# Matmul and layer norm, 2048 x 2048 x 2048: another order for the first chunk's arrivals, and two DMA transposes issued later

## The chip, the cores and the metric

The kernel runs on one core of one Trainium2 chip. The metric is the device time of one execution in microseconds (us). Three runs of the kernel before took 245.06, 245.17 and 246.28 us; the median is 245.17 us.

## The reference

```python
x = np.matmul(a, b)                       # a, b: 2048 x 2048 float32
mean = np.mean(x, axis=-1, keepdims=True)
var = np.var(x, axis=-1, keepdims=True)
normalized = (x - mean) / np.sqrt(var + eps)
return (gamma * normalized + beta).astype(np.float32)
```

The kernel multiplies in fp16 with fp32 sums.

## The kernel before, in words

**Tiles.** The contraction K is cut into 16 tiles of 128, M into 16 row blocks of 128, N into four quarters of 512 columns. One matmul (`mm(i, q, kt, ...)`, L85) takes a 128 x 128 piece of A, transposed, as weights and a 128 x 512 piece of B, and adds into one PSUM bank, so there are 16 x 4 x 16 = 1024 of them. PSUM has 8 banks, which accumulators and transposes share (pool `psum`).

**Opening.** B and the first five row blocks (R = 5, rows 0 to 4) arrive while the matmuls already run. The 16 K tiles come in four chunks of four. For chunk 0 the order is: quarter 0 for all five rows, then quarters 1, 2 and 3. The partial sums of quarters 0, 1 and 2 go aside to SBUF on ScalarE (`put_aside`, L264). Quarter 3 runs on through chunks 1 and 2. Then `part(0, 4, 12, ...)` adds tiles 4 to 11 of quarter 0, and VectorE adds the set-aside sums (`add_part`, L268), which frees the banks. `part(1, ...)` does tiles 4 to 15 of quarter 1: tiles 4 to 11 tile by tile over the five rows, then tiles 12 to 15 row by row. `part(2, ...)` does the same for quarter 2. Later the last chunk of quarters 3 and 0 follows, and then rows 5 to 15, one after the other.

**Arrivals.** Every load is fp32 into a staging buffer (pool `stg`, 6 buffers of 128 x 1024) and is then cast to fp16. Chunk 0 of rows 0 to 4 (called A0 to A4; `load_a1`, cast at L186) and tiles 0 to 3 of B in quarter 0 (B0 to B3; `load_b1`, cast at L199) come as nine loads of 256 KB, in the order of the list `arrivals` (L163). All later B comes two tiles at a time, 512 KB (`load_b2`, cast at L205): B6/1 below is the load of tiles 6 and 7 in quarter 1. The casts are on VectorE, for the list `later` (L349) on ScalarE. All these loads are issued by SyncE (SP), in program order. VectorE also works in program order: an `add_part` stands behind the casts of B4/1 and B6/1.

**Transposing A.** Rows 0 to 4 are turned for chunks 0 to 2 on TensorE (`turn`, four 128 x 128 transposes a row, L252, then a ScalarE copy, L254). For chunk 3, `turn_last(i)` (L258) has SP issue a DMA transpose from SBUF to SBUF; T0 to T4 below are those of rows 0 to 4. Their weights are first used by tiles 12 to 15 of `part(1, ...)`. Rows 5 and up are transposed whole by DMA (L346).

**Order around the change.** The order of TensorE's work in chunk 0 is written out by hand (L276 to L294): filler matmuls on zeros, each row's `turn` just after its arrival, and the matmuls between. SP's order behind the opening's loads is B4/1, B6/1, T0, T1, B8/1, T2, T3, B10/1, T4, B12/1, B14/1, B4/2, B6/2 and so on (L349 to L359).

Of the kernel before, what the change touches and what calls it, by code (L numbers as in the profile page):

```python
# [16 lines left out]
def kernel(  # L17
# [19 lines left out]
    KC = 4  # L37
    KW = KC * P
    n_kc = n_kt // KC
    R = 5  # L40
# [32 lines left out]
    def bank(name):  # L73
        return psum.tile([P, NB], FP32, tag="ps", name=name)
# [4 lines left out]
    def at(i):  # L79
        return pair[i // 2][:, i % 2]  # L80

    def mm(i, q, kt, first, last):
        if (i, q) not in acc:
            acc[i, q] = bank(f"acc{i}_{q}")
        nc.tensor.matmul(  # L85
            acc[i, q], at(i)[:, kt, :], b16[:, kt, ds(q * NB, NB)],
            start=first, stop=last,
        )
# [71 lines left out]

    arrivals = [("a", 0), ("b", 0)] + [("a", i) for i in range(1, R)]  # L163
    arrivals += [("b", k) for k in range(1, KC)]

    a16_of = {}
    fresh = {"st": 0}
# [33 lines left out]
    def load_b2(k, q, cast=nc.vector.tensor_copy):  # L201
        st = stg.tile([P, 2, NB], FP32, tag="st", name=f"stb{q}_{k}")
        nc.sync.dma_start(
            st, b[ds(k * P, 2 * P), ds(q * NB, NB)].rearrange("(t p) n -> p t n", p=P))
        cast(b16[:, k:k + 2, ds(q * NB, NB)], st)  # L205
        return st
# [36 lines left out]
    def filler(n, to=None):  # L243
        for _ in range(n):
            nc.tensor.matmul(warm if to is None else to, zeros[:, 0:P], zeros, start=True, stop=True)  # L245

    def turn(rows, c):
        n = len(rows)
        t_ps = psum.tile([P, n, KC, P], FP16, tag="ps", name=f"tps{rows[0]}_{c}")
        for m, i in enumerate(rows):  # L250
            for j in range(KC):
                nc.tensor.transpose(t_ps[:, m, j, :], a16_of[i, c][:, ts(j, P)], ident)  # L252
        i0 = rows[0]
        nc.scalar.copy(  # L254
            pair[i0 // 2][:, ds(i0 % 2, n), ds(c * KC, KC), :], t_ps)

    def turn_last(i):
        nc.sync.dma_start_transpose(at(i)[:, ds(K3, KC), :], a16_of[i, n_kc - 1])  # L258

    def put_aside(p, q):  # L260
        if xs[p] is None:
            xs[p] = xpool.tile([P, N], FP32, tag="x", name=f"x{p}")
            bnst[p] = stat.tile([P, n_nb, 6], FP32, tag="bnst", name=f"bnst{p}")
        nc.scalar.copy(xs[p][:, ds(q * NB, NB)], acc.pop((p, q)))  # L264
# [15 lines left out]
    filler(1)  # L280
    turn([1], 0)
    filler(2)
    for i in range(2, R):
        turn([i], 0)
        mm(i - 1, 0, 0, True, False)
    for p in range(R - 1):
        mm(p, 0, 1, False, False)
    mm(R - 1, 0, 0, True, False)
    mm(R - 1, 0, 1, False, False)
    for kt in range(2, KC):  # L290
        for p in range(R):
            mm(p, 0, kt, False, kt == KC - 1)
            if kt == KC - 1:
                put_aside(p, 0)  # L294


    for q in ASIDE[1:]:
# [40 lines left out]
    def load_row(i):  # L338
        a16[i] = a16p.tile([P, K], FP16, tag="a16", name=f"a16_{i}")
        nc.gpsimd.dma_start(a16[i], a[ts(i, P), :])  # L340
# [9 lines left out]
    later += [(k, 2) for k in range(KC, n_kt, 2)]  # L350
    later += [(k, q) for q in (MAIN, 0) for k in range(K3, n_kt, 2)]
    for n, (k, q) in enumerate(later):
        for i in range(2 * n, min(2 * n + 2, R)):
            turn_last(i)
        st = load_b2(k, q, nc.scalar.copy)
        if (k, q) in ((n_kt - 2, 2), later[-1]):
            nc.gpsimd.tensor_copy(gate, st[:, 0, 0:1])
        if (k, q) == (n_kt - 2, 2):
            load_row(R)  # L359
# [152 lines left out]
```

## Time and profile before

| what | value |
|---|---|
| time, median of 3 runs | 245.17 us |
| the profiled execution's own time | 244.29 us |
| its span, first to last instruction | 242.2 us |
| mean granted TensorE clock | 0.993 |
| matmuls of L85 | 1024 |
| VectorE busy, share of the span | 71% |
| ScalarE busy, share of the span | 27% |
| `at<-a16s` DMA transposes, issue to landing | 6.4 us median (5.7 to 7.1) |
| `stb<-in_b_dram` loads of 512 KB, issue to landing | 7.1 us median (4.5 to 9.6) |

A profile has one row for a group of instructions: start, length, engine, line, operation, output and input, count, and in brackets how long the engine sat idle before and what ended that. Matmul rows overlap: one lasts 0.38 us by the profile, but the next starts long before it ends. So a row of n matmuls lasts n - 1 steps from start to start and 0.38 us more, and a wait shows as a step that is too long.

### The profile page before, as it was taken

To read this page: it belongs to the slowest core of one execution; us is meant where nothing else is said; L and a number is where in the kernel's file an instruction comes from. 1 tells how busy PE (TensorE), PEld (TensorE's weight loads), DVE (VectorE), ACT (ScalarE), POOL (GpSimd) and SP (SyncE) were. 2 spreads that over 40 slices of the span, in tenths; PEclk is the share of its full clock that TensorE was granted. 3 is DMA by queue.
4 is the path that set the end of the run, shared out by engine and by line. 5 is a ranking of instruction groups with operands and counts; after the bars stand their busy time and mean duration, and the time that the engine had idled before them with its cause. 6 is when DMAs were issued, how large, how long until landed. Compare 5 with 4: busy or idle time off the path is not lost.

```text
span 242.2 us, 2970 instructions
## 1 busy us (share of the span) xinstructions
PE 235.4 (97%) x1117; PEld 107.5 (44%) x1117; DVE 171.6 (71%) x300; ACT 66.0 (27%) x115; POOL 12.5 (5%) x20
## 2 busy tenths in 40 slices
PE   7999999999999999999999999999999999999992
PEld 2444554444444444444444444444444444444441
DVE  1554545606359998999999999998858392946761
ACT  2465443146760013020202103112111121112132
POOL 0000000000120001000000000004500000000000
PEclk9999999999999999999999999999999999999997
DMA  5999999999979999948898978999927145130405
GB/s 123 396 387 387 386 384 374 195 344 387 381 137 203 346 209 180 238 180 185 247 229 225 248 162 293 236 201 186 228 81 183 76 117 145 53 120 1 173 0 173
DMA packets 43909, 53.28 MB, mean 220 GB/s; under 512 B 27124, under 2 KB 27124, under 8 KB 43640
## 3 DMA queue, kind: packets, MB, share of 16 engines
q1 hardware_dynamic: 42312, 47.34, 63.7%
q0 software_dynamic: 1584, 5.77, 14.8%
q8 instruction: 8, 0.13, 0.2%
q14 instruction: 5, 0.04, 0.0%
HBM read 35.67 MB, written 16.78 MB: 217 GB/s over the span
## 4 chain that ended last, share of the span: by engine, by line
PE 94%; DMA 2%; ACT 1%; DVE 1%; issue 0%; DVEq 0%
PE acc L85 91%; DMA st<-in_a_dram 2%; PE tps L252 2%; PE warm L245 1%; ACT x L437 1%; DVE bnst L402 0%; DVE x L268 0%; PE y L425 0%; DVE a16s L186 0%; PE ms_ps L420 0%; ACT mv_last L418 0%; DVE mv_last L417 0%; ACT lead L421 0%; DVEq L268 0%
## 5 line engine op out<-in xcount | busy, mean ns | idle before, releaser
L85 PE MATMUL acc<-b,at 128*128 128x512 f16 x1024 | 223.0, 379 | 0.1
L85 PEld LDWEIGHTS <-at 128*128 128x128 f16 x1024 | 99.8, 98 | 120.2 <-ACT at L254 1.1
L96 DVE BATCH_NORM_STATS2 bnst<-x 128x6 f32<-128x512 f32 x43 | 29.4, 687 | 23.0 <-ACT x L95 23.0
L117 DVE SCALAR_TENSOR_TENSOR x<-x,rstd,beta_b 128x512 f32<-128x512 f32 x62 | 44.4, 756 | 0.6
L111 DVE SCALAR_TENSOR_TENSOR x<-x,mv,gamma_b 128x512 f32<-128x512 f32 x60 | 42.9, 756 | 0.0
L95 ACT COPY x<-acc 128x512 f32<-128x512 f32 x43 | 24.5, 585 | 66.9 <-PE acc L85 66.9
L272 DVE TENSOR_TENSOR x<-acc,x 128x512 f32<-128x512 f32 x20 | 13.6, 678 | 13.6 <-PE acc L85 13.6
L106 ACT ACTIVATE sq<-ve 128x1 f32<-128x1 f32 x15 | 3.0, 203 | 65.2 <-DVE ve L104 65.2
L205 DVE CAST b<-stb 128x1024 f16<-128x1024 f32 x16 | 11.1, 694 | 12.5 <-DMA stb<-in_b_dram 12.5
L205 ACT CAST b<-stb 128x1024 f16<-128x1024 f32 x14 | 14.6, 1045 | 16.8 <-DMA stb<-in_b_dram 16.8
L273 DVE BATCH_NORM_STATS2 bnst<-x 128x6 f32<-128x512 f32 x20 | 13.9, 694 | 0.7
L264 ACT COPY x<-acc 128x512 f32<-128x512 f32 x20 | 10.2, 605 | 7.5 <-PE acc L85 7.5
L254 ACT COPY at<-tps 128x512 f16<-128x512 f16 (+1 forms) x11 | 8.1, 742 | 10.8 <-PE tps L252 10.5
L340 POOL DMA_DIRECT2D a<-in_a_dram x11 | 6.0, 548 | 92.9 <-DMA at<-a 92.1
L245 PE MATMUL warm<-zeros 128*128 128x512 f16 x19 | 7.4, 534 | 1.2 <-DVE zeros L152 1.2
L186 DVE CAST a16s<-st 128x512 f16<-128x512 f32 x8 | 3.4, 428 | 5.9 <-DMA st<-in_a_dram 5.7
L194 DVE CAST a16s<-sta 128x1024 f16<-128x1024 f32 x6 | 4.2, 694 | 4.1 <-DMA sta<-in_a_dram 3.4
L386 POOL TENSOR_SCALAR gb<-gb 1x1024 f32<-1x1024 f32 x2 | 5.6, 2829 | 0.0
L252 PEld LDWEIGHTS <-a16s 128*128 128x128 f16 x60 | 4.0, 100 | 3.6 <-DVE a16s L186 2.2
L252 PE MATMUL tps<-ident,a16s 128*128 128x128 f16 x60 | 5.4, 225 | 0.1
L102 DVE BATCH_NORM_AGGREGATE mv<-bnst 128x2 f32<-128x24 f32 x15 | 4.0, 264 | 0.5
L245 PEld LDWEIGHTS <-zeros 128*128 128x128 f16 x19 | 2.2, 127 | 3.9 <-issue 2.5
(33 smaller groups left out, 26.3 us busy)
## 6 DMA issues: line engine op xcount, KB each, us to landing
stb<-in_b_dram SPq DMA_DIRECT2D x30, 512.0 KB, 7.1
out_dram<-x SPq DMA_DIRECT2D x30, 512.0 KB, 4.3
a<-in_a_dram POOLq DMA_DIRECT2D x11, 512.0 KB, 6.2
sta<-in_a_dram SPq DMA_DIRECT2D x6, 512.0 KB, 6.5
st<-in_a_dram SPq DMA_DIRECT2D x8, 256.0 KB, 6.1
st<-in_b_dram SPq DMA_DIRECT2D x4, 256.0 KB, 6.0
gamma_b<-in_gamma_dram SPq DMA_DIRECT2D x1, 1024.0 KB, 5.5
beta_b<-in_beta_dram SPq DMA_DIRECT2D x1, 1024.0 KB, 8.6
```

Of the source, the lines that this page charges most:

```text
L85: nc.tensor.matmul(acc[i, q], at(i)[:, kt, :], b16[:, kt, ds(q * NB, NB)], start=first, stop=last,)
L95: nc.scalar.copy(xs[i][:, qs], acc[i, q])
L96: nc.vector.bn_stats(bnst[i][:, q, :], xs[i][:, qs])
L111: nc.vector.scalar_tensor_tensor(xs[i][:, qs], xs[i][:, qs], mv[:, 0:1], gamma_b[:, qs], AluOp.subtract, AluOp.mult)
L117: nc.vector.scalar_tensor_tensor(xs[i][:, qs], xs[i][:, qs], rstd, beta_b[:, qs], AluOp.mult, AluOp.add)
L205: cast(b16[:, k:k + 2, ds(q * NB, NB)], st)
L245: nc.tensor.matmul(warm if to is None else to, zeros[:, 0:P], zeros, start=True, stop=True)
L252: nc.tensor.transpose(t_ps[:, m, j, :], a16_of[i, c][:, ts(j, P)], ident)
L254: nc.scalar.copy(pair[i0 // 2][:, ds(i0 % 2, n), ds(c * KC, KC), :], t_ps)
L264: nc.scalar.copy(xs[p][:, ds(q * NB, NB)], acc.pop((p, q)))
L272: nc.vector.tensor_tensor(xs[p][:, qs], acc[p, q], xs[p][:, qs], AluOp.add)
L273: nc.vector.bn_stats(bnst[p][:, q, :], xs[p][:, qs])
```

## The change

The nine first loads come in the order A0 B0 A1 A2 A3 B1 B2 A4 B3 instead of A0 B0 A1 A2 A3 A4 B1 B2 B3. TensorE's hand-written order follows: the matmuls of rows 0 to 3 on tiles 1 and 2 stand before row 4's `turn`, and row 4 does its four matmuls last. SP issues T0, B8/1, T1, B10/1, T2, B12/1, B14/1, T3, T4, B4/2, so that at most one transpose stands between two loads of quarter 1, and T3 and T4 stand behind the last of them. The number of instructions of every kind is the same.

```diff
-    arrivals = [("a", 0), ("b", 0)] + [("a", i) for i in range(1, R)]
-    arrivals += [("b", k) for k in range(1, KC)]
+    arrivals = [("a", 0), ("b", 0)] + [("a", i) for i in range(1, R - 1)]
+    arrivals += [("b", 1), ("b", 2), ("a", R - 1), ("b", 3)]
...
-    for i in range(2, R):
+    for i in range(2, R - 1):
         turn([i], 0)
         mm(i - 1, 0, 0, True, False)
+    for p in range(R - 2):
+        mm(p, 0, 1, False, False)
+    for kt in (0, 1):
+        mm(R - 2, 0, kt, kt == 0, False)
+    for p in range(R - 2):
+        mm(p, 0, 2, False, False)
+    turn([R - 1], 0)
+    mm(R - 2, 0, 2, False, False)
     for p in range(R - 1):
-        mm(p, 0, 1, False, False)
-    mm(R - 1, 0, 0, True, False)
-    mm(R - 1, 0, 1, False, False)
-    for kt in range(2, KC):
-        for p in range(R):
-            mm(p, 0, kt, False, kt == KC - 1)
-            if kt == KC - 1:
-                put_aside(p, 0)
+        mm(p, 0, 3, False, True)
+        put_aside(p, 0)
+    for kt in range(KC):
+        mm(R - 1, 0, kt, kt == 0, kt == KC - 1)
+    put_aside(R - 1, 0)
...
     for n, (k, q) in enumerate(later):
-        for i in range(2 * n, min(2 * n + 2, R)):
+        for i in {0: (0,), 1: (1,), 2: (2,), 4: (3, 4)}.get(n, ()):
             turn_last(i)
```

## The prediction

> **What bounds the kernel now.** I read the page first, then the chain that ended last in order of time, then the timelines of single engines at the two places the change touches.
>
> ```profile
> PE 235.4 (97%) x1117; PEld 107.5 (44%) x1117; DVE 171.6 (71%) x300; ACT 66.0 (27%) x115; POOL 12.5 (5%) x20
> ```
>
> TensorE sets the time. Only its waits can be won, so I looked for those in the chain:
>
> ```profile
> 46.50 0.69 DVE x L268
> ...
> 47.24 8.36 PE acc L85 x38
> 55.60 0.04 issue
> 55.64 177.59 PE acc L85 x822
> ```
>
> From 9.97 us to the end of the matmuls at 233.23 us the chain leaves TensorE twice only: at 47.24, which an `add_part` released, and at 55.64. The timeline of TensorE sizes the two waits:
>
> ```profile
> 13.25 11.17 PE L85 MATMUL acc<-b,at 128*128 128x512 f16 x51
> 46.56 1.05 PE L85 MATMUL acc<-b,at 128*128 128x512 f16 x3
> 55.00 1.01 PE L85 MATMUL acc<-b,at 128*128 128x512 f16 x3
> ```
>
> The first row is undisturbed: 50 steps in 11.17 - 0.38 us, 0.216 us a matmul. In the second, two steps take 0.67 instead of 0.43: a wait of 0.24 us before the start at 47.24. In the third, two steps take 0.63: a wait of 0.20 us before 55.64. Counting 0.216 us a matmul from the last `turn` (its chain piece ends at 32.70) puts `part(1)`, row 4, tile 4 at 47.24 and row 0, tile 14 at 55.64. What they waited for:
>
> ```profile
> 42.46 0.69 DVE L205 CAST b<-stb 128x1024 f16<-128x1024 f32 x1 [0.81 <-DMA stb<-in_b_dram]
> 45.29 0.69 DVE L205 CAST b<-stb 128x1024 f16<-128x1024 f32 x1 [2.14 <-DMA stb<-in_b_dram]
> 45.90 3.08 DVE L268 TENSOR_TENSOR x<-acc,x 128x512 f32<-128x512 f32 x5
> ```
> ```profile
> 54.54 1.04 ACT L205 CAST b<-stb 128x1024 f16<-128x1024 f32 x1 [0.75 <-DMA stb<-in_b_dram]
> ```
>
> The bank for row 4 is freed by the second of five adds (46.50 to 47.18). VectorE could have begun the adds when row 0 was summed, about 44.6, but stood 2.14 us waiting for B6/1, whose cast is ahead of them. At 55.64 tile 14 had waited for the cast of B14/1, which ended at 55.58. So both waits come from the B stream, and SP's rows show what stands in it:
>
> ```profile
> 37.67 2.70 SPq L258 DMA_TRANSPOSE at<-a16s  x2
> 40.47 0.53 SPq L203 DMA_DIRECT2D stb<-in_b_dram  x1
> 41.09 4.46 SPq L258 DMA_TRANSPOSE at<-a16s  x2
> 45.60 0.58 SPq L203 DMA_DIRECT2D stb<-in_b_dram  x1
> ```
>
> **Part 1, the opening.** VectorE's casts and TensorE's rows:
>
> ```profile
> 9.09 0.43 DVE L186 CAST a16s<-st 128x512 f16<-128x512 f32 x1 [0.27 <-DMA st<-in_a_dram]
> 9.76 0.43 DVE L199 CAST b<-st 128x512 f16<-128x512 f32 x1 [0.24 <-DMA st<-in_b_dram]
> 10.43 0.43 DVE L199 CAST b<-st 128x512 f16<-128x512 f32 x1 [0.25 <-DMA st<-in_b_dram]
> 11.11 0.43 DVE L199 CAST b<-st 128x512 f16<-128x512 f32 x1 [0.25 <-DMA st<-in_b_dram]
> ```
> ```profile
> 9.29 0.39 PE L85 MATMUL acc<-b,at 128*128 128x512 f16 x1
> 9.57 0.40 PE L252 MATMUL tps<-ident,a16s 128*128 128x128 f16 x4
> 9.95 0.39 PE L85 MATMUL acc<-b,at 128*128 128x512 f16 x1
> ```
>
> The nine loads are alike (256 KB, one every 0.67 us, casts of 0.43 us for A and B), so I let the slots keep their times and change only who sits in them: B1 9.09, B2 9.76, A4 10.43, B3 11.11. Until 9.29 (row 2, tile 0) nothing changes. Before: 9.29, `turn` of row 4 at 9.57, row 3 at 9.95, then row 0, tile 1 at 10.23 (B1's cast ended at 10.18) and 15 more steps of 0.216, so quarter 1 starts at 10.23 + 16 x 0.2156 = 13.68. After: row 0, tile 1 at 9.57 (the slot's cast ends at 9.52, as A4's did for the start at 9.57). From there 17 matmuls and one `turn` follow; eight transposes with nothing waiting move the chain by 0.45 (24.64 to 25.09), so four cost 0.22. 9.57 + 17 x 0.2156 + 0.22 = 13.46. **Gain 0.23 us.** The feeds come in time: B2 cast 10.18, used 10.65; A4 cast 10.86, `turn` 11.30; B3 cast 11.54, used 11.73; row 4's ScalarE copy (0.59, begun 0.2 after the `turn`) ends about 12.3, used 12.59. The set-asides move from 13.02 to about 12.3, nothing waits longer. Quarter 1's first B is cast by 13.17, 0.29 before use. If the slots swap less kindly, a load late by 0.1 costs 0.1 at most 0.23 before the gain is gone.
>
> **Part 2, the B stream.** The order of SP changes, the work does not. The trace's semaphores go round in eight, each transfer waiting for the one eight before. B6/1 was issued at 37.25, T0 follows; B8/1 moves from 40.47 to 39.0, B10/1 from 45.60 to about 41, B12/1 and B14/1 from 47.5 and 48.1 to 43 to 44. T3 must wait for B6/1's landing, about 45, T4 follows, both out by 48; B4/2 is queued behind them, 48 against 48.7 now. T3 and T4 take 5.7 to 7.1 us to land: 52 to 55, while row 3's tile 12 comes at about 57. That slack of 2 us or more hides the move; without it every us late costs one.
>
> When does B14/1 land? Casts started, so loads landed, at 45.29, 47.77 (T0 and T1 between), 50.12 (T2, T3), 52.75 (T4), 54.54, 56.68, then every 1.34. So a transpose costs the stream (2.48 - 1.34)/2 = 0.57 or (2.35 - 1.34)/2 = 0.51, in the worst row 1.29. With three instead of five: 45.1 + 4 x 1.34 + 3 x 0.55 = 52.1, or 54.3 with 1.29 each. Needed is 53.85 (use at 54.96, less 1.04 and 0.06). I take 52.1, since two of three rows lie there. **The wait of 0.20 goes.**
>
> The Trainium skill (Advanced Engine Details and Errata, X-Bar Transpose) says that transposing DMAs run as fast as plain ones, 350 to 400 GB/s; for 128 KB that is an estimate of 0.35 us, and B14/1 would come only 0.7 us earlier, just enough. The rows above say more than 0.5 each.
>
> **B6/1 itself**, the hard term: T0 still follows it, only T1 goes. Bounds: it lands as now (45.29), or as the loads before it did (42.46 + 1.34 = 43.8). In the trace 15 of its 16 completion counts came by 43.72 and the last at 45.27; a code fetch (queue q8, 16 KB) began at 42.28 and took 2.20 us, where the one at 21.39 took 1.05. The fetch follows TensorE's position, 0.23 earlier after the change. I take the row that the last count is nearest to: B6/1 lands about 0.2 earlier, 45.05. Then the wait at 47.24 stays at 0.24 and passes the opening's gain on.
>
> The Trainium skill (DMA: Bandwidth & Descriptors, Queues, rings and completion order) says that a completion count lands only after all earlier writes of its DMA engine, across queues. By that rule the late count hangs on the fetch and not on T1, which is the reading taken here; no row shows which engine made the fetch.
>
> **Sum.** 0.23 + 0.20 = 0.43 us: 244.29 becomes 243.86 for the profiled execution. That one lies 0.88 below the median; on the median, 245.17 - 0.43 = 244.7.
>
> **The rivals.**
> 1. T1 was what held B6/1: it lands by 44.8, both waits go: 0.23 + 0.24 + 0.20 = 0.67, 244.5. For it: packets stood still around T0 and T1 alone, T2 to T4 cost 0.5. Against: the last count and the fetch.
> 2. B6/1 lands at 45.29 whatever comes behind: row 4, tile 4 stays at 47.24, the opening's gain is swallowed there, and 0.20 is left: 245.0. For it: loads before B6/1 keep their places, so nothing upstream moves.
> 3. Slower: each transpose standing alone between loads holds the stream as T0 did. B4/1 to B6/1 took 2.83, 1.49 over 1.34. Three such: 45.05 + 5.36 + 3 x 1.49 = 54.9, and tile 14 starts at 56.0 against 55.64: slower by 0.4, 245.6; with a second hold of 1.5 as at a fetch, 1.9, 247.1. It decides from a landing of B14/1 after 54.54; each us beyond is a us. Against: T1 to T4 cost about 0.5.
> 4. The change does nothing in the opening: B1 in A4's slot lands later by 0.2 or more. Then 0.20 to 0.0, 245.1.
>
> **Numbers.** Forecast 0.42, rival 1 0.22, rival 2 0.13, rival 3 0.13, rival 4 0.06, and 0.04 for a larger gain where timed executions hold longer at B6/1 than the profiled one. Predicted 244.7. The range takes in the bounds 244.5 and 245.1 and the first half of rival 3, and below the forecast as much again as the runs scatter: 244.1 to 245.8. A measurement tells about 0.5% (1.2 us) from no change. No case but the last and the far end of rival 3 passes it: faster 0.08, same 0.83, slower 0.09.
>
> **What would show it.** Right: quarter 1's first matmul at 13.46; no ScalarE cast just before a late step near 55; VectorE's fifth-last cast before the adds starting near 45.05; TensorE's last matmul 0.43 earlier. Wrong: B14/1's cast starting after 54.5, a step over 0.22 in `part(1)` rows 3 and 4 (T3, T4 late), or a wait between 9.6 and 13.4.

## The result, and the profile after

The changed kernel took 244.25 us, the median of 22 runs (243.69 to 245.38); the kernel before took 245.12 beside it (22 runs, 244.2 to 246.39). The ratio is 0.9968, with a 95% interval of 0.9954 to 0.9982: 0.8 us less, 0.4 to 1.1 by the interval. It was compared twice more below (0.9982, 0.9963 to 1.0001, and 0.9983, 0.9960 to 1.0006). Weighted by their intervals the three give 0.9975, about 0.6 us, with some 0.25 to either side if they are taken as independent. That is under 0.5%, to the faster side, as forecast; 0.43 us had been worked out. The median of the kernel before differs from one comparison to the next (244.45 to 245.12 in the four made here) by as much as the change is worth, so only ratios to runs taken beside it are used.

The profile that came with the result is of an execution at the upper end of its runs: 245.38 us, span 242.9 us. Its first line:

```profile
PE 234.3 (96%) x1117; PEld 107.2 (44%) x1117; DVE 171.2 (70%) x300; ACT 65.9 (27%) x115; POOL 12.7 (5%) x20
```

The casts of the opening on VectorE, in the changed order, and TensorE's rows beside them:

```profile
9.04 0.43 DVE L186 CAST a16s<-st 128x512 f16<-128x512 f32 x1 [0.25 <-DMA st<-in_a_dram]
9.72 0.43 DVE L199 CAST b<-st 128x512 f16<-128x512 f32 x1 [0.25 <-DMA st<-in_b_dram]
10.40 0.43 DVE L199 CAST b<-st 128x512 f16<-128x512 f32 x1 [0.25 <-DMA st<-in_b_dram]
11.05 0.43 DVE L186 CAST a16s<-st 128x512 f16<-128x512 f32 x1 [0.23 <-DMA st<-in_a_dram]
11.71 0.43 DVE L199 CAST b<-st 128x512 f16<-128x512 f32 x1 [0.23 <-DMA st<-in_b_dram]
```
```profile
9.53 0.40 PE L252 MATMUL tps<-ident,a16s 128*128 128x128 f16 x4
9.92 2.16 PE L85 MATMUL acc<-b,at 128*128 128x512 f16 x9
11.92 0.39 PE L252 MATMUL tps<-ident,a16s 128*128 128x128 f16 x4
```

The slots are 0.67 us apart as before, with B1 and B2 in the sixth and seventh and A4 in the eighth. The whole row of casts is 0.63 us later than in the profile of before (9.72 against 9.09 for the sixth), because B0 was cast later, at 7.01 instead of 6.37. So this profile can only be read from its own first loads. From 9.92 TensorE does nine matmuls, row 4's `turn` and the next matmuls without a gap, and quarter 1 starts at 14.09: 4.37 us after the sixth cast starts, where it was 13.68 - 9.09, or 4.60 unrounded, before.

Later, in the chain that ended last, and on VectorE and ScalarE at that place:

```profile
46.84 1.29 DVE x L268 x2
48.13 0.04 issue
48.17 185.79 PE acc L85 x860
```
```profile
21.20 0.69 DVE L194 CAST a16s<-sta 128x1024 f16<-128x1024 f32 x1 [0.66 <-DMA sta<-in_a_dram]
24.10 0.69 DVE L205 CAST b<-stb 128x1024 f16<-128x1024 f32 x1 [2.20 <-DMA stb<-in_b_dram]
...
44.85 0.69 DVE L205 CAST b<-stb 128x1024 f16<-128x1024 f32 x1 [0.75 <-DMA stb<-in_b_dram]
46.23 0.69 DVE L205 CAST b<-stb 128x1024 f16<-128x1024 f32 x1 [0.68 <-DMA stb<-in_b_dram]
46.84 3.08 DVE L268 TENSOR_TENSOR x<-acc,x 128x512 f32<-128x512 f32 x5
```
```profile
48.48 1.04 ACT L205 CAST b<-stb 128x1024 f16<-128x1024 f32 x1 [9.56 <-DMA stb<-in_b_dram]
50.04 1.04 ACT L205 CAST b<-stb 128x1024 f16<-128x1024 f32 x1 [0.51 <-DMA stb<-in_b_dram]
51.84 1.04 ACT L205 CAST b<-stb 128x1024 f16<-128x1024 f32 x1 [0.75 <-DMA stb<-in_b_dram]
53.23 1.04 ACT L205 CAST b<-stb 128x1024 f16<-128x1024 f32 x1 [0.35 <-DMA stb<-in_b_dram]
```

The chain leaves TensorE once instead of twice: the wait at row 0, tile 14 is gone, since B14/1's cast, the last of the four on ScalarE (B8/1, B10/1, B12/1, B14/1), starts at 53.23 and tile 14 is only reached after 56. The wait behind the adds is still there, and longer: 0.39 us at row 3, tile 4 and 0.38 at row 4. B6/1 came 1.38 us behind B4/1 (46.23 - 44.85), as plain loads do, against 2.83 before. But the whole stream of loads was late in this execution: behind the cast at 21.20 the next load took 2.9 us to come, where before it took 1.35 and the one after it was held up, for less. From the sixth cast to B6/1's it took 36.51 us here and 36.20 before. That is 0.31 more, TensorE is 0.23 earlier, and the wait of 0.24 should grow to 0.78; the two waits are 0.77 together.

### The profile page after: what moved, and what is told of

The parts are those of the page before. It is cut to its first block, busy times and chain, and to the rows that moved or that the text cites. A ratio compares the mean times of both kernels' runs of the same rounds, so it can differ in the third digit from the quotient of the medians.

```text
span 242.9 us, 2971 instructions
## 1 busy us (share of the span) xinstructions
PE 234.3 (96%) x1117; PEld 107.2 (44%) x1117; DVE 171.2 (70%) x300; ACT 65.9 (27%) x115; POOL 12.7 (5%) x20
## 4 chain that ended last, share of the span: by engine, by line
PE 93%; DMA 2%; DVE 1%; ACT 1%; SPq 0%; issue 0%; DVEq 0%
PE acc L85 91%; DMA st<-in_a_dram 2%; PE tps L252 1%; ACT x L442 1%; DVE x L268 1%; DVE bnst L407 0%; PE y L430 0%; DVE a16s L186 0%; PE warm L245 0%; SPq L198 0%; SPq L184 0%; PE ms_ps L425 0%; ACT mv_last L423 0%; DVE mv_last L422 0%; ACT lead L426 0%
## 5 line engine op out<-in xcount | busy, mean ns | idle before, releaser
L85 PE MATMUL acc<-b,at 128*128 128x512 f16 x1024 | 223.0, 379 | 1.5 <-DVE b L199 1.0
L85 PEld LDWEIGHTS <-at 128*128 128x128 f16 x1024 | 99.7, 98 | 120.5 <-issue 1.2
L117 DVE SCALAR_TENSOR_TENSOR x<-x,rstd,beta_b 128x512 f32<-128x512 f32 x62 | 43.9, 748 | 0.6
L245 PE MATMUL warm<-zeros 128*128 128x512 f16 x19 | 6.5, 476 | 1.2 <-DVE zeros L152 1.2
L194 DVE CAST a16s<-sta 128x1024 f16<-128x1024 f32 x6 | 4.2, 694 | 4.1 <-DMA sta<-in_a_dram 4.1
```

The costliest lines, as they stand in the source:

```text
L85: nc.tensor.matmul(acc[i, q], at(i)[:, kt, :], b16[:, kt, ds(q * NB, NB)], start=first, stop=last,)
L117: nc.vector.scalar_tensor_tensor(xs[i][:, qs], xs[i][:, qs], rstd, beta_b[:, qs], AluOp.mult, AluOp.add)
```

## The experiments

Each was timed in five rounds beside the kernel before, and gave one profile. Three numbers are read from every profile: the time from the start of the sixth cast to quarter 1's first matmul; the time from the start of the cast of rows 2 and 3's chunk 3 (L194, at 39.13 before) to the start of B6/1's cast, four loads later; and TensorE's waits behind quarter 1's first matmul, at tile 4 of rows 3 and 4 and at tile 14 of row 0 (a step less than 0.03 us too long counts as none). The second column says whether the opening, and then the order of the transposes, is the old or the new one.

| kernel | opening, order | sixth cast | to quarter 1 | to B6/1 | waits (row 3, row 4, tile 14) | ratio and interval |
|---|---|---|---|---|---|---|
| before | old, old | 9.09 | 4.60 | 6.16 | 0, 0.24, 0.20 | |
| before again | old, old | 9.52 | 4.61 | 6.00 | 0, 0.11, 0.11 | 1.0011 (0.9992 to 1.0031) |
| opening only | new, old | 9.20 | 4.37 | 6.90 | 1.18, 0.38, 0.25 | 1.0005 (0.9989 to 1.0022) |
| order only | old, new | 9.59 | 4.60 | 5.75 | none | 1.0019 (1.0001 to 1.0038) |
| order only, again | old, new | 9.72 | 4.60 | 5.83 | 0, 0.36, 0 | 0.9994 (0.9969 to 1.0019) |
| after | new, new | 9.72 | 4.37 | 6.06 | 0.39, 0.38, 0 | 0.9968 (0.9954 to 0.9982) |
| after, second | new, new | 9.27 | 4.37 | 5.12 | none | 0.9982 (0.9963 to 1.0001) |
| after, third | new, new | 8.95 | 4.37 | 5.38 | none | 0.9983 (0.9960 to 1.0006) |
| T1 back | new, T1 as before | 9.38 | 4.37 | 6.04 | 0.37, 0.38, 0 | 1.0006 (0.9983 to 1.0029) |
| two plain first | new, T0 behind B10/1 | 9.28 | 4.37 | 5.13 | none | 0.9980 (0.9962 to 0.9997) |
| all behind | new, T0 behind B14/1 | 9.22 | 4.37 | 5.35 | 0.27 at row 5 | 0.9998 (0.9977 to 1.0020) |
| two ahead | new, T0, T1 before B6/1 | 9.40 | 4.37 | 7.84 | 1.67, 0.38, 0 | 1.0108 (1.0077 to 1.0139) |
| cast on ScalarE | new, new | 9.29 | 4.37 | 5.34 | none | 0.9971 (0.9952 to 0.9990) |
| opening, cast on ScalarE | new, old | 9.74 | 4.37 | 5.70 | 0, 0, 0.03 | 0.9990 (0.9959 to 1.0021) |

**The two parts, each alone.** The opening alone keeps the old loop:

```diff
-        for i in {0: (0,), 1: (1,), 2: (2,), 4: (3, 4)}.get(n, ()):
+        for i in range(2 * n, min(2 * n + 2, R)):
```

> Only the first part of the change: arrivals and hand-written order of chunk 0; SP's order of the transposes T0 to T4 as before. Measured from the start of the sixth cast (the slot at 9.09 us before), quarter 1's first matmul should come 4.37 us later instead of 4.59, in every theory. Theory F (as predicted: T0 and the code fetch hold B6/1, and the B stream of quarter 1 still carries all five transposes): the 0.23 us is swallowed in part(1), the waits there grow from 0.44 to about 0.67 us, ratio 0.999 to 1.000. Rival W (in the timed executions the waits of part(1) are mostly not there, the profiled one was unlucky): the 0.23 us is kept, ratio about 0.999. Rival G (the gain of the whole change is bigger than its profile shows because the opening gains more in executions whose first loads come late): ratio 0.997.

The opening's gain is there, 4.37, and nothing of it reaches the end: 1.0005. VectorE's rows of this profile:

```profile
43.59 0.69 DVE L205 CAST b<-stb 128x1024 f16<-128x1024 f32 x1 [0.75 <-DMA stb<-in_b_dram]
46.50 0.69 DVE L205 CAST b<-stb 128x1024 f16<-128x1024 f32 x1 [2.21 <-DMA stb<-in_b_dram]
47.11 3.07 DVE L268 TENSOR_TENSOR x<-acc,x 128x512 f32<-128x512 f32 x5
```

B6/1 comes 2.91 us behind B4/1 as in the profile of before (2.83), and TensorE, which is earlier, waits longer: 1.81 us in all. It is the swallowing that theory F foresaw. Its 0.67 us of waits is too little for this execution, which is the slowest of its runs (246.28 us). The order alone is the kernel before with the new loop:

> Only the second part: SP's order T0, B8/1, T1, B10/1, T2, B12/1, B14/1, T3, T4; the opening as before. Theory F: the wait for B14/1 (0.20 us before) goes, the wait for B6/1 (0.24) stays: 0.2 us, ratio 0.9992, and no step over 0.22 us near part(1), row 0, tile 14. Rival 1 (T1 held B6/1): both waits go, 0.44 us, ratio 0.998. Rival 3 (a transpose alone between loads holds the stream like the first one): B14/1's cast starts after 54.5 and the ratio is over 1.000.

Its profile has no wait: the chain runs from the last `turn` to the last matmul without leaving TensorE,

```profile
33.21 200.09 PE acc L85 x927
```

where before the same 927 matmuls ended at 233.23 from 32.70, 200.53 us: 0.44 more. Yet the runs were no faster: 1.0019, with an interval that lies just above 1. So it was run again.

> The second part alone once more, since its first run (1.0019, 1.0001 to 1.0038) went against its own profile, which has no wait in part(1). Theory T (two transposes one right behind the other are what held B6/1, by about 1 us, so the new order takes the waits away): B4/1 to B6/1 under 2.3 us, no wait in part(1), ratio 0.998. Rival O (the order gains nothing by itself, since with the old opening TensorE reaches part(1) 0.23 us later and its waits are shorter in most executions): ratio 0.999 to 1.000. Rival S (the new order costs something later that the profile of the first run did not hold): ratio 1.002 again, and a wait somewhere after part(1).

0.9994 this time, with one wait of 0.36 us. Weighted as above, the two together give 1.0010 (0.9995 to 1.0025), so at most 0.05% faster. The wait after `part(1)` that rival S asks for was not found. Little was to be expected by the profiles themselves: the two of the order alone have 0 and 0.36 us of waits, the two of the kernel before 0.44 and 0.22, 0.15 us more on average, which makes a ratio of 0.9994. What the order alone is worth in the timed runs is not settled; 0.2% faster, rival 1's figure for it, is not borne out.

**The changed kernel again, and the kernel before again.**

> The changed kernel as it is, for a second profile and on the same chip as the others. Theory F: quarter 1's first matmul 4.37 us after the sixth cast starts, waits in part(1) of 0.2 to 0.3 us at row 4, tile 4 and none at row 0, tile 14; ratio 0.998. Rival 1: no wait at either, ratio 0.997. Rival N (the waits at row 3 and row 4, tile 4, 0.77 us together, of the changed kernel's first profile are its rule, since T0 to T2 hold the issue of the loads): the same waits again, ratio near 1.000.

No wait at all: both waits of before are gone, which was rival 1's case. Its chain:

```profile
32.65 200.09 PE acc L85 x927
```

Rival N falls: the 0.77 us of the first profile is not the rule. The kernel before against itself:

> The kernel before, against itself: what the intervals are worth, and a second profile of it. Every theory: ratio 1.000 with an interval of about 0.002 to both sides. Theory T: B4/1 to B6/1 about 2.8 us, waits in part(1) of 0.4 us, or some 1.0 to 1.6 us where the B stream was held up at 21 us. Theory F: B4/1 to B6/1 anywhere between 1.3 and 2.8, by where the code fetch falls.

The interval holds 1.000. But B6/1 came 1.32 us behind B4/1 (44.30 to 45.62), with T1 right behind T0. Theory T, as put, falls: two transposes in a row do not always hold B6/1 for 1.5 us. The delay of this execution came in one place earlier:

```profile
39.62 0.69 DVE L194 CAST a16s<-sta 128x1024 f16<-128x1024 f32 x1 [0.63 <-DMA sta<-in_a_dram]
41.68 0.69 DVE L205 CAST b<-stb 128x1024 f16<-128x1024 f32 x1 [1.36 <-DMA stb<-in_b_dram]
```

The second row started 1.32 us after the first in the profile of before and 2.06 us here. This is why the table counts over all four loads.

**T1 alone put back, and fewer transposes near B6/1.** On the changed kernel, T1 ahead of B8/1 again; or T0 and T1 behind B10/1; or all five behind B14/1:

```diff
-        for i in {0: (0,), 1: (1,), 2: (2,), 4: (3, 4)}.get(n, ()):
+        for i in {0: (0, 1), 2: (2,), 4: (3, 4)}.get(n, ()):
...
+        for i in {2: (0, 1), 4: (2, 3, 4)}.get(n, ()):
...
+        for i in {4: (0, 1, 2, 3, 4)}.get(n, ()):
```

> The changed kernel with T1 alone put back behind T0, ahead of B8/1; T2 to T4 stay where the change put them. Theory T (T1 right behind T0 is what made B6/1 late): B4/1 to B6/1 2.8 us again, the code fetch near 43 us takes over 2 us again, and the wait at row 4, tile 4 is back with 0.4 us or more; ratio 0.999 to 1.000, worse than the changed kernel by 0.2 to 0.4%. Theory F (T0 and the fetch, T1 does not matter): as the changed kernel, B4/1 to B6/1 1.4 to 2.3, ratio 0.998.

> The changed kernel with no transpose until B10/1 is out: B6/1, B8/1, B10/1, then T0, T1, B12/1, B14/1, then T2, T3, T4. Theory T: B4/1 to B6/1 1.3 us as in the run with all five behind, no wait in part(1), as good as the changed kernel or up to 0.2 us better on average; ratio 0.997 to 0.998. Rival L (what the five transposes take must be paid somewhere): a wait at tile 14 of row 0 near 55, or at the start of row 5 near 81 as in the run with all five behind (0.27 us), ratio 0.999 to 1.000.

> The changed kernel, with all five transposes issued behind B14/1, so that B6/1 to B14/1 come as plain loads. Theory F (T0 itself is what holds B6/1): B6/1 lands about 1.3 us after B4/1, both waits of part(1) go, 0.67 us less than before, ratio 0.997, some 0.25 us better than the changed kernel. Rival 1 (T1 held B6/1, T0 does not): no better than the changed kernel. Rival L (five in a row behind the loads land late): T0 lands after its use at row 0, tile 12, about 54.5, and a step there is too long by what it is late; slower than the changed kernel.

With T1 back the wait is back, 0.75 us, and the ratio is 1.0006, though B4/1 to B6/1 was 1.33 and the code fetch took 1.04 us: the result of theory T without its two marks. Against the three comparisons of the changed kernel (0.9975) it is 0.31% slower, with some 0.25 to either side. With T0 and T1 behind B10/1 nothing waits (0.9980). With all five behind, B6/1 comes as a plain load, but the last loads slip, and row 5's transpose lands late, as the chain of that kernel shows:

```profile
63.89 7.98 DMA a<-in_a_dram
71.87 0.02 issue
71.89 8.90 DMA at<-a
80.79 0.05 issue
80.84 152.13 PE acc L85 x704
```

TensorE waited 0.27 us there for `at` of row 5. The wait that rival L named, T0 late for tile 12 of row 0, did not come. What holds of it is that the time of the transposes is paid elsewhere, here at row 5.

**The suspected cost enlarged, and the wait taken away.** In one kernel T0 and T1 go ahead of B6/1, whose cast stays on VectorE. In two others, the changed kernel and the opening alone, B6/1's cast goes to ScalarE with SP's order kept. In all three the load moves into the list `later`, in front, and the places of the transposes in that list move with it (not shown):

```diff
-    load_b2(KC + 2, 1)
...
-    later = [(k, 1) for k in range(2 * KC, n_kt, 2)]
+    later = [(k, 1) for k in range(KC + 2, n_kt, 2)]
```

> The changed kernel with T0 and T1 issued ahead of B6/1 instead of behind it: the suspected cost enlarged. Theory B (what the change won hangs on when B6/1 lands, a microsecond for a microsecond, and each transpose ahead of it costs about 0.5 us): the cast of B6/1 starts some 0.5 to 1.5 us later against the loads before it than in the changed kernel, the waits at row 3 and row 4, tile 4 are 1 us or more together; ratio 1.002 to 1.004. Rival H (B6/1's landing hardly matters in timed executions, the opening's 0.23 us and the first loads make the difference): ratio 0.998.

> The changed kernel with the cast of B6/1 on ScalarE, which has nothing to do then, so that the adds that free the banks no longer stand behind it on VectorE; SP's order is the same. Theory B: no wait at row 3 and row 4, tile 4, even where B6/1 lands late; never worse than the changed kernel, on average up to 0.3 us better; ratio 0.996 to 0.998. Rival H: as the changed kernel.

> The new opening with the old order of the transposes, and the cast of B6/1 on ScalarE. Theory B: no wait at tile 4 any more, so the opening's gain gets through to tile 14 of row 0; there B14/1, behind five transposes, still makes TensorE wait 0.2 to 0.7 us. Ratio 0.998 to 1.000: better than the opening alone (1.0005), not as good as with the new order. Rival H: 0.998, no wait matters.

> The changed kernel a third time, beside the other three. Every theory: ratio 0.997 to 0.998. Theory B: the wait in part(1), if there is one, is the start of B6/1's cast plus 1.91 us, less the time at which row 4, tile 4 could have run.

Two transposes ahead made it slower by 1.1% (0.8 to 1.4), more than the 0.2 to 0.4% expected. VectorE's rows:

```profile
43.27 0.69 DVE L205 CAST b<-stb 128x1024 f16<-128x1024 f32 x1 [0.81 <-DMA stb<-in_b_dram]
47.19 0.69 DVE L205 CAST b<-stb 128x1024 f16<-128x1024 f32 x1 [3.23 <-DMA stb<-in_b_dram]
```

VectorE stood 3.23 us with the adds behind that cast, and TensorE waited 2.05 us in all. The profiled execution is one of the quicker of its runs (246.13 us, of 245.84 to 249.88), so these waits are less than the 2.6 us between the medians. Rival H falls: a late B6/1 reaches the end. With the cast on ScalarE the adds start without it, in the changed kernel as soon as row 0 is summed:

```profile
43.67 0.69 DVE L205 CAST b<-stb 128x1024 f16<-128x1024 f32 x1 [0.75 <-DMA stb<-in_b_dram]
44.66 3.08 DVE L267 TENSOR_TENSOR x<-acc,x 128x512 f32<-128x512 f32 x5 [0.29 <-PE acc L85]
```

The bracket of the adds now names TensorE: VectorE waits for it, and no longer the other way round. No wait is left, 0.9971. Beside it the third run of the changed kernel had 0.9983; the two intervals overlap almost wholly, so that this version is better than the changed one is not shown. On the opening alone it takes both waits at tile 4 away, and 0.03 us at tile 14 is left (0.9990, which cannot be told from 1 or from 0.998).

## Why the prediction was right, and where not

**The opening, 0.23 us: right.** In all ten profiles with the new opening quarter 1 begins 4.37 us after the sixth cast starts, in all four with the old one 4.60. Swapping A and B loads between slots cost nothing, so rival 4 falls.

**That the gain need not reach the end: right.** The opening alone measures 1.0005, and in the first profile of the changed kernel the gain is swallowed at B6/1, as in rival 2. The arithmetic of the wait holds in every profile that has B6/1's cast on VectorE: row 4, tile 4 starts 1.91 us (cast, first add, second add) and some 0.03 after B6/1's cast starts, or when TensorE reaches it, whichever is later. For the profiles with a wait that gives 47.23 (before), 47.56 (before again), 48.44 (opening only), 48.17 (after), 48.00 (order only, again), 47.81 (T1 back) and 49.13 (two ahead); measured were 47.24, 47.56, 48.45, 48.17, 48.00, 47.81 and 49.13.

**The wait at tile 14, 0.20 us: right.** It is 0.03 to 0.25 in the four profiles with the old order and in none with T3 and T4 behind B14/1. The forecast had B14/1 landing at 52.1 and the second profile of the changed kernel, whose B4/1 lands as in the profile of before, casts it at 51.25. T3 and T4 were never waited for.

**B6/1, the step that was mis-sized.** The prediction took it to land 0.2 us earlier and the wait at 47.24 to stay. From the cast of rows 2 and 3 to B6/1's it is 6.00 to 6.90 us with the old order, or 5.70 where B6/1 is cast on ScalarE (mean of four 6.19); 5.12 to 6.06 with T0 alone behind B6/1 (mean of six 5.58); 5.13 and 5.35 with no transpose there. So by the means T1 costs B6/1 about 0.6 us and T0 another 0.3, not 0.2 and nothing. With T1 put back alone it is 6.04. The single executions differ by as much as the means do: the 0.6 has a standard error of about 0.3, and the 0.3 rests on two profiles without a transpose. That points to rival 1's mechanism, and in two of three profiles of the changed kernel its outcome is there, both waits gone. These two are of executions quicker than the medians beside them (243.85 and 243.43 us against 244.16 and 244.44), and the one with waits is the slowest of its 22, so how often the waits are gone is not known. One profile of each kernel would have shown the waits growing from 0.44 to 0.77.

The reason the prediction gave for its choice, that the last completion count of B6/1 hung on the code fetch, is not borne out as the whole. The fetch near 43 us took 2.20 and 2.56 us in the two profiles with the old order in which B6/1 came over 2.8 us behind B4/1, and 0.94 to 1.15 in the other twelve. So the long fetch and the late count go together with T1 behind T0, in two profiles of five that had it so; which of them holds the other was not tried. Nor did the fetch move with TensorE's position, 0.23 us earlier, as the forecast took it: in every profile TensorE runs from quarter 1 to past 46 us without a wait, but this fetch began 33.1 to 34.2 us after the sixth cast, on average 33.6 with the old opening and 33.7 with the new.

**The sum.** Forecast 0.43; three comparisons together say about 0.6, their interval reaches to under 0.4, and 0.67 was rival 1's sum. Two things fit the larger value: B6/1's 0.6 us, and that both profiled executions of before (244.29 and 244.41 us) were quicker than the medians beside them, so their waits of 0.44 and 0.22 are likely too small for a common run. That second point is argued, not shown, and the same can be said of the two profiles of the changed kernel without a wait. That 244.25 lies in the range says little: the range is 1.7 us wide and takes in the sums of rivals 1, 2 and 4. Open is the order alone, whose timed runs did not show a gain.

**The signs.** Counted from the sixth cast, the last matmul of L85 ends after 224.12 us before, and after 224.23, 223.46 and 223.48 us in the three profiles of the changed kernel. Where no wait is left it is 0.66 and 0.64 us earlier: the opening's 0.23 and both waits, not 0.43. The sign of being wrong "a step over 0.22 in `part(1)` rows 3 and 4" did come in the first profile, but at tile 4 and released by the adds, not by T3 or T4. And "VectorE's fifth-last cast before the adds" should read the last: that is B6/1's.

**Rival 3** (a transpose alone between loads holds the stream as T0 did) did not come. In the first profile after the change B6/1, B8/1, B10/1, B12/1 and B14/1 were cast 2.25, 1.56, 1.80 and 1.39 us apart, with T0, T1 and T2 alone in the first three spaces: 0.91, 0.22 and 0.46 us over the 1.34 of a plain load, not 1.49 each. From B6/1 to B14/1 the three together took 1.51 to 1.66 us over plain loads in all six profiles with the new order. So the forecast's 3 x 0.55 was right, though the first of them takes over half of it; and in the second profile B14/1 was cast 0.85 us ahead of the forecast because B6/1 was 0.80 ahead. The Trainium skill's rate (Advanced Engine Details and Errata, X-Bar Transpose (TRN2): as fast as plain DMAs, an estimate of 0.35 us for 128 KB, so 1.05 for three) is too quick here: the trace agrees with the forecast's 0.55. It does not cover what T0 and T1 did to B6/1 either.

## What to carry to other kernels

An engine that works in order passes a late load on to everything behind it: here five adds that freed banks stood behind a cast that did not concern them, and when that cast could run decided whether a gain thirty microseconds earlier reached the end. Before moving a step, find the next place where the engine meets the load stream and subtract: what reaches the end is what was won, less what the wait there grows by. With effects of 0.2%, compare profiles from a mark inside each (here a cast) and take several: the first pair of profiles pointed the wrong way.

## What the runs showed of the hardware

- The first loads land with a scatter of their own: the sixth of nine casts starts between 8.95 and 9.74 us in fourteen profiles, whatever the order.
- A code fetch of 16 KB (queue q8) begins between 21 and 23 us in every profile. Soon after, and until about 31 us, the last of the sixteen completion counts of each load trails the fifteenth by 0.8 to 1.7 us in all fourteen (before: 22.58 for the fifteenth, 23.63 for the last); ahead of the fetch it was 0.45 us or less. As a load is there only with its last count, the stream behind is late by that much; the 2.20 us in VectorE's row at 24.10 above is such a place. The fetch is the only thing seen at that time; that it is the cause was not tried.
- The sixteen counts of the load just ahead of the first DMA transpose mostly come nearly at one moment (after: B6/1's between 46.11 and 46.21), while those of B4/1 just before were spread from 42.40 to 44.83. With T0 and T1 ahead of B6/1 it is B4/1's counts that come together (43.13 to 43.24), and where no transpose stands behind B6/1 its counts spread over 1.8 and 2.0 us. Why is not shown. In before and in the opening alone the counts came in two bunches 1.5 us apart, so it is not simply that all wait for the last one.
- A DMA transpose alone between two 512 KB loads held the second of them back by 0.80 to 0.93 us (T0, the first), 0.21 to 0.27 (T1) and 0.45 (T2), in the six profiles with the new order.
